# Transposing the recurrence's values step by step into a ring, and sharing slots between tiles

## The chip, the cores and the metric

The kernel runs on one core of one Trainium2 chip. The metric is the device time of one execution in microseconds. A core has five engines that each work through a queue of their own in order: TensorE (PE; its weight loads are shown as PEld), VectorE (DVE), ScalarE (ACT), GpSimd (POOL) and SyncE (SP), which here issues the weight transfers. Data lie in SBUF, in 128 partitions; matmuls write to PSUM, which has eight banks.

## What is computed

The reference runs four blocks over 256 latent tokens and 256 context tokens of width 1024, all in float32. The change touches the first one (layer 0): a modulated norm, an input projection, a mixer of differential attention and an RWKV recurrence, an output projection, and a squared-ReLU MLP, for latent and context tokens. The recurrence is run over the context first, forwards and backwards, and its two end states start that over the latent tokens:

```python
def step(S, inp):
    r_t, w_t, k_t, v_t, kk_t, a_t = inp
    sa = jnp.einsum('bhvk,bhk->bhv', S, kk_t)
    S = (S * w_t[:, :, None, :] - sa[..., None] * (kk_t * a_t)[:, :, None, :]
         + v_t[..., None] * k_t[:, :, None, :])
    return S, jnp.einsum('bhvk,bhk->bhv', S, r_t)
...
x = x + g1_l * (o_l.astype(x.dtype) @ w_out)
x = x + g2_l * _sq_relu_mlp(_ada(x, norm2, sh2_l, sc2_l), mlp_w1, mlp_w2)
if need_ctx:
    ctx = ctx + g1_c * (o_c.astype(ctx.dtype) @ w_out)
    ctx = ctx + g2_c * _sq_relu_mlp(_ada(ctx, norm2, sh2_c, sc2_c), mlp_w1, mlp_w2)
```

The context result goes on into layer 1; the following two blocks work on the latent tokens alone.

## The kernel before

Activations lie with their features on the partitions and 256 tokens along the row. A large product is three matmuls in a row for each 128x128 block of weights (`mm3`, lines 219 to 221): weights and activations are split into a high part in the format fp32r and a remainder, and high x high, high x low and low x high are added in PSUM. The weights come in pieces of 128x1024 (`w`, four buffers), which ScalarE rounds (`hi`, line 44) and VectorE subtracts (`lo`, line 45), 512 columns at a time.

The recurrence is computed in chunks of 64 tokens, two directions at once. `mixer(s)` in `layer0` is one call of it, for the context (s = 0) and for the latent tokens (s = 1). It has three parts. `rwkv_prep` makes decays and keys. `rwkv_inverse` builds a triangular 64x64 system for each chunk and head and solves it: a loop of 31 rounds of two dependent VectorE instructions (lines 456 and 458), with short matmuls before and after. Then come four steps: `rwkv_pre(j)` prepares step j without the state (exponentials, transposed keys `tok`, masked products `za` and `zr`), and `rwkv_step(j)` uses and updates the state `S`. `pre(j + 1)` is written ahead of `step(j)`. Last, `rwkv_out` and `rwkv_post` norm and gate the result for each of four feature tiles. `rwkv_values` transposes all values ahead of the first step: for each of four feature tiles and two directions it copies a tile into `vx` in chunk order, transposes it on TensorE, and copies the halves into `uv`, which holds all four chunks. A step writes its own results to the other half of `uv`.

In the order of the program layer 0 goes: context input projection, `mixer(0)`'s prep, latent norm, attention, `mixer(0)`'s rest, latent input projection with the token shift (`shifts`), context output projection (`w_out` on `xc`), `mixer(1)`, the context MLP, then the latent output projection (`w_out` on `xl`, with the operands of the latent MLP made in passing, `mlp_enter`), and, in layer 1, the latent MLP. Two MLPs (the latent ones of layers 0 and 1) run their first seven blocks on activations that are not yet normed; one block of the norm is made after each of these (`early` in `mlp`).

The instructions of each engine are put in order before the run, by a scheduler. It takes an instruction when its inputs, its engine and the memory of its output are free, and among several the one that stands first in the program; the first norm of an MLP has a raised priority. Memory is handed out in pools, from both ends of SBUF: in `mixer(1)` the pools `pl`, `q2` (keys, decays), `qx` (`X`, `vx`) and `up` (all of the steps) lie one above the other from below, `xc`, `xl` and then the MLP's pool from above. A pool is placed when it is opened, in the order of the program. Where it covers bytes of a pool that was closed, its tiles wait until the old tiles are done with. Within a pool, tiles with one tag share that tag's slots (`bufs`, one if not given) in turn, and a slot is as large as the largest of them. PSUM has three tags: `mm` (two banks), `sc` (two) and `po` (four).

Of the kernel before, what the change touches and what calls it, by code (L numbers as in the profile page):

```python
# [17 lines left out]
P = 128  # L18
# [57 lines left out]
class Kern:  # L76
# [114 lines left out]
        self.last = nc.scalar.activation(r, r, AF.Exp, scale=-0.5)  # L191
        return r

    def sumsq(self, pool, tiles, T, ones="ones", tag="sc"):

        nc = self.nc
        acc = None
        for t in tiles:
            sq = pool.tile([P, T], F32, tag="sq", name="sq", bufs=2)
            nc.scalar.activation(sq, t, AF.Square)  # L200
            if acc is not None:
                nc.vector.tensor_tensor(sq, sq, acc, op=ALU.add)
            acc = sq
        ps = self.psum(tag)
        nc.tensor.matmul(ps[:, :T], lhsT=self.C(ones), rhs=acc, start=True, stop=True)
        return ps[:, :T]
# [289 lines left out]

    HALF = [slice(0, 64), slice(64, 128)]

    def rwkv_values(self, vp, uv, v):

        nc = self.nc
        for p in range(4):
            for d in range(2):
                vx = vp.tile([P, 4, 64], F32, tag="vx", name="vx")
                lv = self.loc(v[p], d)
                x4 = vx.rearrange("p (a b) i -> p a b i", b=2)
                for b in range(2):
                    nc.vector.tensor_copy(x4[:, :, b, :], lv[:, :, 1 - b, :])
                pt = self.psum("sc")
                for a in range(2):  # L510
                    nc.tensor.transpose(pt[:, 128 * a : 128 * a + 128], vx[:, 2 * a : 2 * a + 2, :].rearrange("p c i -> p (c i)"), self.C("ident"))
                pv = pt[:, 0:256].rearrange("p (c x) -> p c x", x=128)
                for hf in range(2):
                    s = self.HALF[1 - hf]
                    nc.scalar.copy(uv[s, d, hf : 4 : 2, p, :], pv[s])

    def rwkv_pre(self, up, j, r, k, kk, ka, L):

        nc = self.nc
        g = lambda n, shape, bufs=2: up.tile([P] + shape, F32, tag=n, name=n, bufs=bufs)  # L520
        tok, zr, ar, za, el = g("tok", [2, 4, 128]), g("zr", [2, 4, 128]), g("ar", [2, 4, 128]), g("za", [4, 128]), g("el", [2, 4])
        for d, c in enumerate((j, 3 - j)):
            now, other = self.HALF[c & 1], self.HALF[1 - (c & 1)]
            loc = lambda t: t[:, :, 64 * c : 64 * c + 64][:, :, ::-1] if d else t[:, :, 64 * c : 64 * c + 64]
            lv = L[d][:, :, 64 * c : 64 * c + 64]
            ep, en = g("ep", [4, 65], 2), g("en", [4, 64], 1)
            nc.gpsimd.memset(ep[:, :, 0:1], 1.0)
            nc.scalar.activation(ep[:, :, 1:65], lv, AF.Exp)
            nc.scalar.activation(en, lv, AF.Exp, scale=-1.0)
            nc.gpsimd.tensor_copy(el[:, d, :], ep[:, :, 64])  # L530
            bk, A = g("bk", [4, 128], 1), ar[:, d]
            nc.vector.tensor_tensor(bk[:, :, now], loc(ka), en, op=ALU.mult)
            nc.gpsimd.tensor_tensor(A[:, :, other], loc(r), ep[:, :, 1:65], op=ALU.mult)
            nc.vector.tensor_tensor(bk[:, :, other], loc(k), en, op=ALU.mult)
            nc.vector.tensor_tensor(A[:, :, now], loc(kk), ep[:, :, 0:64], op=ALU.mult)
            pt = self.psum("sc")
            for p in range(4):
                nc.tensor.transpose(pt[:, 128 * p : 128 * p + 128], bk[:, p, :], self.C("ident"))
            nc.scalar.copy(tok[:, d], pt.rearrange("p (c x) -> p c x", c=4))
            pz = [self.psum("sc").rearrange("p (x c i) -> p x c i", x=2, c=4) for _ in range(2)]  # L540
            for p in range(4):
                for h, s in enumerate(self.HALF):
                    rhs = A[s, p, :].rearrange("p (a b) -> p a b", b=64)
                    nc.tensor.matmul(pz[h][:, :, p, :], lhsT=bk[s, p, :], rhs=rhs if c & 1 else rhs[:, ::-1, :], start=True, stop=True)  # L544
            for h, s in enumerate(self.HALF):
                mask = lambda n, rows: self.C(n)[rows].unsqueeze(1).broadcast_to([rows.stop - rows.start, 4, 64])
                nc.vector.tensor_tensor(za[other, :, s], pz[h][other, 1], mask("strict", other), op=ALU.mult)
                nc.vector.tensor_tensor(zr[:, d, :, s], pz[h][:, 0], mask("incl", slice(0, 128)), op=ALU.mult)
        return tok, zr, ar, za, el

    def rwkv_step(self, up, j, pre, uv, X, S, sy):


        nc = self.nc
        tok, zr, ar, za, el = pre
        ch = (j, 3 - j)

        ks, vs = [self.HALF[c & 1] for c in ch], [self.HALF[1 - (c & 1)] for c in ch]
# [11 lines left out]
        for q in range(2):  # L570
            for m, h, d in mhd:
                p, hs = 2 * q + m, self.HALF[h]
                nc.tensor.matmul(pp[q][ks[d], cols(d, m)][:, hs], lhsT=za[vs[d], p, hs], rhs=uv[vs[d], d, ch[d], p, hs],
                                 start=False, stop=True, skip_group_check=True)
            t = up.tile([P, 256], F32, tag="pn", name="pn", bufs=2)
            nc.scalar.mul(t[ks[0]], pp[q][ks[0], both(0)], -1.0)
            nc.vector.tensor_scalar(t[ks[1]], pp[q][ks[1], both(1)], -1.0, None, op0=ALU.mult)
            pn.append(t)
        for q in range(2):
            ps = self.psum("po")  # L580
            for m, h, d in mhd:
                i = (q * 2 + h) * 8 + (m * 2 + d) * 2 + ch[d] // 2
                o = slice(128 * m + 64 * h, 128 * m + 64 * h + 64)
                nc.tensor.matmul(ps[ks[d], o], lhsT=X[ks[d], i, :], rhs=pn[q][ks[d], o], start=True, stop=True, skip_group_check=True)
            for d in range(2):
                (nc.vector.tensor_copy if d else nc.scalar.copy)(uv[ks[d], d, ch[d], 2 * q : 2 * q + 2, :], ps[ks[d], 0:256].rearrange("p (m x) -> p m x", m=2))
        for q in range(2):
            ps = self.psum("po")
            pv = ps.rearrange("p (d m x) -> p d m x", m=2, d=2)
            for m, d in md:  # L590
                p = 2 * q + m
                nc.tensor.matmul(pv[:, d, m], lhsT=tok[:, d, p, :], rhs=uv[:, d, ch[d], p, :], start=True, stop=True, skip_group_check=True)
            for hs in self.HALF:
                s, e = S[hs, :, 2 * q : 2 * q + 2, hs], el[hs, :, 2 * q : 2 * q + 2]
                nc.vector.tensor_tensor(s, s, pv[hs, :, :, hs], op=ALU.add)
                nc.vector.tensor_tensor(s, s, e.unsqueeze(3).broadcast_to([64, 2, 2, 64]), op=ALU.mult)
        for q in range(2):
            for m, h, d in mhd:
                p, hs = 2 * q + m, self.HALF[h]
                nc.tensor.matmul(pp[q][vs[d], cols(d, m)][:, hs], lhsT=zr[:, d, p, hs], rhs=uv[:, d, ch[d], p, hs],  # L600
                                 start=False, stop=True, skip_group_check=True)
            for d in range(2):
                nc.scalar.copy(sy[vs[d], j, 256 * q : 256 * q + 256], pp[q][vs[d], both(d)])
# [16 lines left out]
    def rwkv_post(self, pool, y, r, k, v, gd, lora, p):  # L620
# [7 lines left out]
        d = pool.tile([P, 256], F32, tag="en", name="yd", bufs=1)  # L628
        nc.vector.scalar_tensor_tensor(d, ps[:, 0:256], -1.0 / 64, y, op0=ALU.mult, op1=ALU.add)
        nc.vector.tensor_tensor(t, ps[:, 256:512], v, op=ALU.mult)  # L630
        q = self.rstd(pool, self.sumsq(pool, [d], 256, "blk"), 64, 256, 2)
        nc.vector.tensor_tensor(d, d, q, op=ALU.mult)
        nc.vector.tensor_scalar(d, d, self.V("lnx_w")[:, p : p + 1], self.V("lnx_b")[:, p : p + 1], op0=ALU.mult, op1=ALU.add)
        nc.gpsimd.tensor_tensor(d, d, t, op=ALU.add)
# [4 lines left out]
    def layer0(self):  # L639
# [14 lines left out]
        mk = lambda n: [[g(pools[s], f"{n}{i}") for i in range(4)] for s in range(2)]  # L654
        v, oa = mk("v"), mk("oa")

        r4, k4 = [[g(pools[s], n, (P, 4, 256)) for s in range(2)] for n in ("r", "k")]
        r, k = [[[t[:, i, :] for i in range(4)] for t in x] for x in (r4, k4)]
# [18 lines left out]
        def mixer(s):  # L677
            with ExitStack() as D:
# [6 lines left out]
                    X = self.rwkv_inverse(pool("rp", E), qx, kk, ka, L)  # L685
                yield
                up = pool("up", D)
                uv, sy = g(up, "uv", (P, 2, 4, 4, 128)), g(up, "sy", (P, 4, 512))
                pre = lambda j: self.rwkv_pre(up, j, r4[s], k4[s], kk, ka, L)
                nxt = pre(0)  # L690
                self.rwkv_values(qx, uv, v[s])
                for j in range(4):
                    now, nxt = nxt, pre(j + 1) if j < 3 else None
                    self.rwkv_step(up, j, now, uv, X, S, sy)
# [105 lines left out]
    def mlp(self, l, mp, x, w, sm, h=None, done=None, side=(), tags=("mm", "mm")):  # L800
# [14 lines left out]
        for i in range(parts):  # L815
            u = []
            for n in range(m):
# [3 lines left out]
                b0 += 8  # L821
                if n % 4 == 2:
                    next(side, None)
                r = mp.tile([P, 256], F32, tag="relu", name="relu", bufs=2)
                if i == 0 and n < NF:
                    b = mp.tile([P, 1], F32, tag="bias", name="bias", bufs=2)
                    nc.vector.tensor_copy(b, ps[:, 256:257])
# [1002 lines left out]
```

## Time and profile before

| | us |
|---|---|
| median of 3 runs | 2097.12 (2091.21 to 2104.70) |
| the profiled execution | 2099.59 |
| its span, first to last instruction | 2097.8 |
| TensorE busy | 1928.2 |
| VectorE busy | 1425.8 |
| ScalarE busy | 1163.7 |
| GpSimd busy | 276.1 |

The profile is of one execution. A busy time is the time in which at least one instruction of that engine is on record as running; matmuls overlap, so their mean duration is longer than the distance at which they follow each other. Lines such as L45 are lines of the kernel before. A group of instructions is named by the tile written and the tiles read, `lo<-w,hi`. Each fp32 matmul shows as two records. The granted clock is TensorE's, as a share of 2.4 GHz; its other level is 1.2 GHz, shown as 0.50.

### The profile page before, as it was taken

To read this page: it belongs to the slowest core of one execution; us is meant where nothing else is said; L and a number is where in the kernel's file an instruction comes from. 1 tells how busy PE (TensorE), PEld (TensorE's weight loads), DVE (VectorE), ACT (ScalarE), POOL (GpSimd) and SP (SyncE) were. 2 spreads that over 40 slices of the span, in tenths; PEclk is the share of its full clock that TensorE was granted. 3 is DMA by queue.
4 is the path that set the end of the run, shared out by engine and by line. 5 is a ranking of instruction groups with operands and counts; after the bars stand their busy time and mean duration, and the time that the engine had idled before them with its cause. 6 is when DMAs were issued, how large, how long until landed. Compare 5 with 4: busy or idle time off the path is not lost.

```text
span 2097.8 us, 42380 instructions
## 1 busy us (share of the span) xinstructions
PE 1928.2 (92%) x16330; PEld 1739.4 (83%) x16330; DVE 1425.8 (68%) x2978; ACT 1163.7 (55%) x2543; POOL 276.1 (13%) x407
## 2 busy tenths in 40 slices
PE   5999999936989999999988989999999999999997
PEld 2986668715779999989855969999889999879997
DVE  3765866675666668557577988666777665677654
ACT  2554563533355568556463857666665555555553
POOL 1421120121010000000131030000003210103210
PEclk8999999965989999999998999999999999999999
DMA  8532541600025555676447515655424554224553
GB/s 280 169 120 72 180 138 35 205 28 1 1 93 182 184 184 193 223 241 206 150 146 236 175 67 167 193 188 183 161 92 140 182 185 167 81 101 141 182 187 114
DMA packets 91785, 313.26 MB, mean 149 GB/s; under 512 B 10304, under 2 KB 17728, under 8 KB 91584
## 3 DMA queue, kind: packets, MB, share of 16 engines
q1 hardware_dynamic: 83376, 299.94, 43.3%
q10 hardware_dynamic: 8208, 10.63, 1.6%
q8 instruction: 128, 2.10, 0.4%
q14 instruction: 73, 0.60, 0.1%
HBM read 309.48 MB, written 1.05 MB: 148 GB/s over the span
## 4 chain that ended last, share of the span: by engine, by line
PE 73%; DVE 11%; DMA 6%; ACT 5%; issue 2%; POOL 2%; ACTq 0%; POOLq 0%; SPq 0%; DVEq 0%
PE mm L219 15%; PE mm L220 15%; PE mm L221 15%; PE po L221 3%; PE po L220 3%; PE po L219 3%; DMA w<-in_mlp 2%; DMA w<-in_w_in 2%; DMA w<-in_mod 2%; PE sc L544 2%; PE mm L150 1%; DVE lo L45 1%; PE po L1391 1%; PE po L568 1%; ACT hi L44 1%
## 5 line engine op out<-in xcount | busy, mean ns | idle before, releaser
L45 DVE TENSOR_TENSOR lo<-w,hi 128x512 fp32r<-128x512 f32 x948 | 651.5, 693 | 294.6 <-ACT hi L44 272.4
L44 ACT CAST hi<-w 128x512 fp32r<-128x512 f32 x948 | 575.8, 618 | 425.0 <-PE mm L220 282.7
L219 PE MATMUL mm<-u_h,hi 128*128 128x256 f32 x1120 | 315.5, 282 | 4.0 <-ACT u_h L212 3.6
L220 PE MATMUL mm<-u_l,hi 128*128 128x256 f32 x1120 | 315.5, 282 | 0.2
L221 PE MATMUL mm<-u_h,lo 128*128 128x256 f32 x1120 | 315.2, 282 | 0.0
L219 PEld LDWEIGHTS mm<-u_h,hi 128*128 128x128 f32 x1120 | 212.6, 190 | 6.3 <-ACT u_h L212 4.0
L220 PEld LDWEIGHTS mm<-u_l,hi 128*128 128x128 f32 x1120 | 211.8, 189 | 0.5 <-DVE u_l L213 0.5
L221 PEld LDWEIGHTS mm<-u_h,lo 128*128 128x128 f32 x1120 | 211.9, 189 | 0.0
L150 PE MATMUL mm<-w,cs 128*32 128x256 f32 x640 | 70.6, 460 | 29.9 <-DMA w<-in_mod 29.6
L252 POOL TENSOR_SCALAR hf<-hf,g,mT 128x256 f32<-128x256 f32 x24 | 21.1, 879 | 473.8 <-ACT h1h L251 384.9
L1596 POOL TENSOR_TENSOR ut<-ut,gt 128x256 f32<-128x256 f32 x44 | 54.0, 1226 | 197.8 <-ACT hi L44 173.6
L150 PEld LDWEIGHTS mm<-w,cs 128*32 128x32 f32 x640 | 18.5, 118 | 60.1 <-DMA w<-in_mod 39.3
L213 DVE TENSOR_TENSOR u_l<-relu,u_h 128x256 fp32r<-128x256 f32 x96 | 40.7, 425 | 34.4 <-ACT u_h L212 34.4
L343 POOL TENSOR_SCALAR sht<-shf,mu 128x256 f32<-128x256 f32 x28 | 37.8, 1348 | 112.5 <-ACT shf L341 112.4
L219 PE MATMUL mm<-h0h,hi 128*128 128x256 f32 x130 | 40.2, 312 | 12.2 <-ACT h0h L251 6.1
L212 ACT CAST u_h<-ut 128x256 fp32r<-128x256 f32 x44 | 17.9, 406 | 58.2 <-POOL ut L1596 58.2
L213 DVE TENSOR_TENSOR u_l<-ut,u_h 128x256 fp32r<-128x256 f32 x44 | 18.7, 425 | 43.8 <-ACT u_h L212 43.8
L1548 POOL TENSOR_TENSOR xl<-xl,yy 128x256 f32<-128x256 f32 x16 | 14.2, 890 | 228.9 <-DVE yy L1547 228.9
L219 PEld LDWEIGHTS mm<-h0h,hi 128*128 128x128 f32 x130 | 25.0, 194 | 20.9 <-ACT h0h L251 7.4
L832 ACT ACTIVATE relu<-relu 128x256 f32<-128x256 f32 x96 | 39.9, 417 | 4.0 <-DVE h7l L253 1.5
L221 PE MATMUL mm<-h0h,lo 128*128 128x256 f32 x130 | 38.7, 298 | 3.5 <-DVE lo L45 3.5
L68 POOL TENSOR_TENSOR sq<-sq 128x256 f32<-128x256 f32 x24 | 20.9, 870 | 158.9 <-ACT sq L60 156.5
(1125 smaller groups left out, 6177.1 us busy)
## 6 DMA issues: line engine op xcount, KB each, us to landing
w<-in_mlp SPq DMA_DIRECT2D x192, 512.0 KB, 4.5
w<-in_w_in SPq DMA_DIRECT2D x102, 512.0 KB, 4.1
w<-in_mod SPq DMA_DIRECT2D x96, 512.0 KB, 5.7
w<-in_ffn_in SPq DMA_DIRECT2D x88, 512.0 KB, 3.7
w<-in_ffn_out SPq DMA_DIRECT2D x44, 512.0 KB, 4.5
w<-in_w_out SPq DMA_DIRECT2D x40, 512.0 KB, 4.3
w<-in_memkv SPq DMA_DIRECT2D x8, 512.0 KB, 3.8
xc<-in_ctxT ACTq DMA_DIRECT2D x16, 128.0 KB, 5.9
```

What stands on the lines that cost most here:

```text
L44: nc.scalar.copy(self.hi, w)
L45: nc.vector.tensor_tensor(self.lo, w, self.hi, op=ALU.subtract)
L150: nc.tensor.matmul(ps[32 * j : 32 * j + 32, o : o + 256], lhsT=self.cs[:, k, :], rhs=w[:, 256 * j : 256 * j + 256], start=(k == 0), stop=( ...
L213: nc.vector.tensor_tensor(lo, src, hi, op=ALU.subtract)
L219: nc.tensor.matmul(out, lhsT=wh, rhs=xh, start=start, stop=False)
L220: nc.tensor.matmul(out, lhsT=wh, rhs=xl, start=False, stop=False)
L221: nc.tensor.matmul(out, lhsT=wl, rhs=xh, start=False, stop=stop)
L252: (nc.gpsimd if k % 2 else nc.vector).tensor_scalar(t, t, scale, bias, op0=ALU.mult, op1=ALU.add)
L343: nc.gpsimd.tensor_scalar(t, f[:, 1:257], self.mu1[:, i : i + 1], None, op0=ALU.mult)
L544: nc.tensor.matmul(pz[h][:, :, p, :], lhsT=bk[s, p, :], rhs=rhs if c & 1 else rhs[:, ::-1, :], start=True, stop=True)
L832: nc.scalar.activation(r, r, AF.Square)
L1596: nc.gpsimd.tensor_tensor(w, w, t, op=ALU.mult)
```

## The change

The values are no longer transposed ahead of the steps. `rwkv_values` is gone. `rwkv_pre(j)` copies the values of its own two chunks to `vx`, transposes them in four matmuls into one bank of `sc`, and copies each direction's half to `uv`. `uv` now holds one step's chunks and has two slots in turn. Besides, slots are shared: in the post-work `sq` goes into the slots of `za` and `rstd` into that of `vx`, both in `up`, and the MLP's `relu` goes into the two slots of `hf`. `vx` moves from the pool `qx` to `up`, where it is twice as large. `v` becomes one tile of 128x4x256 for each `s`, of the same size as the four before. Indexing of `uv` by chunk falls away.

```diff
-    def sumsq(self, pool, tiles, T, ones="ones", tag="sc"):
+    def sumsq(self, pool, tiles, T, ones="ones", tag="sc", sq="sq"):
...
-            sq = pool.tile([P, T], F32, tag="sq", name="sq", bufs=2)
-            nc.scalar.activation(sq, t, AF.Square)
+            x = pool.tile([P, T], F32, tag=sq, name="sq", bufs=2)
+            nc.scalar.activation(x, t, AF.Square)
...
-    def rwkv_values(self, vp, uv, v):
-
-        nc = self.nc
-        for p in range(4):
-            for d in range(2):
-                vx = vp.tile([P, 4, 64], F32, tag="vx", name="vx")
-                lv = self.loc(v[p], d)
-                x4 = vx.rearrange("p (a b) i -> p a b i", b=2)
-                for b in range(2):
-                    nc.vector.tensor_copy(x4[:, :, b, :], lv[:, :, 1 - b, :])
-                pt = self.psum("sc")
-                for a in range(2):
-                    nc.tensor.transpose(pt[:, 128 * a : 128 * a + 128], vx[:, 2 * a : 2 * a + 2, :].rearrange("p c i -> p (c i)"), self.C("ident"))
-                pv = pt[:, 0:256].rearrange("p (c x) -> p c x", x=128)
-                for hf in range(2):
-                    s = self.HALF[1 - hf]
-                    nc.scalar.copy(uv[s, d, hf : 4 : 2, p, :], pv[s])
-
-    def rwkv_pre(self, up, j, r, k, kk, ka, L):
+    def rwkv_pre(self, up, j, r, k, v, kk, ka, L):
...
+        uv, vx = g("uv", [2, 4, 128]), g("vx", [4, 128], 1)
         for d, c in enumerate((j, 3 - j)):
...
+            nc.vector.tensor_copy(vx[:, :, other], loc(v))
...
+        pt = self.psum("sc")
+        for p in range(4):
+            nc.tensor.transpose(pt[:, 128 * p : 128 * p + 128], vx[:, p, :], self.C("ident"))
+        for d, c in enumerate((j, 3 - j)):
+            s = self.HALF[1 - (c & 1)]
+            nc.scalar.copy(uv[s, d], pt[s].rearrange("p (c x) -> p c x", c=4))
+        return tok, zr, ar, za, el, uv
...
-        q = self.rstd(pool, self.sumsq(pool, [d], 256, "blk"), 64, 256, 2)
+        q = self.rstd(None, self.sumsq(pool, [d], 256, "blk", sq="za"), 64, 256, 2, pool.tile([P, 256], F32, tag="vx", name="rstd"))
...
-                uv, sy = g(up, "uv", (P, 2, 4, 4, 128)), g(up, "sy", (P, 4, 512))
-                pre = lambda j: self.rwkv_pre(up, j, r4[s], k4[s], kk, ka, L)
+                sy = g(up, "sy", (P, 4, 512))
+                pre = lambda j: self.rwkv_pre(up, j, r4[s], k4[s], v4[s], kk, ka, L)
                 nxt = pre(0)
-                self.rwkv_values(qx, uv, v[s])
                 for j in range(4):
...
-                r = mp.tile([P, 256], F32, tag="relu", name="relu", bufs=2)
+                r = mp.tile([P, 256], F32, tag="hf", name="relu", bufs=2)
```

## Rows read from the trace of the kernel before

**Rows 1.** The page's part 1: busy time, share of the span, instructions.

```profile
PE 1928.2 (92%) x16330; PEld 1739.4 (83%) x16330; DVE 1425.8 (68%) x2978; ACT 1163.7 (55%) x2543; POOL 276.1 (13%) x407
```

**Rows 2.** The page's part 4: shares of the chain that ended last.

```profile
PE 73%; DVE 11%; DMA 6%; ACT 5%; issue 2%; POOL 2%; ACTq 0%; POOLq 0%; SPq 0%; DVEq 0%
```

**Rows 3.** Busy time by stretch: length, PE, PEld, DVE, ACT, POOL (instructions), clock, DMA share, GB/s.

```profile
209.00:260.00 51.00, 47.60 (x322) 33.13 (x320) 45.18 (x138) 28.90 (x76) 7.65 (x10) 1.00 0.55 184
...
294.00:383.00 89.00, 88.10 (x882) 74.71 (x880) 58.19 (x149) 37.37 (x93) 12.32 (x28) 0.96 0.19 62
...
430.00:490.00 60.00, 13.63 (x480) 10.68 (x482) 42.76 (x99) 14.69 (x28) 9.41 (x20) 0.52 0.01 1
455.00:479.00 24.00, 0.00 (x0) 0.00 (x0) 21.84 (x64) 0.00 (x0) 0.00 (x0) 0.50 0.00 0
490.00:590.00 100.00, 85.83 (x797) 70.71 (x792) 58.04 (x151) 38.36 (x97) 11.46 (x28) 0.77 0.01 1
...
590.00:604.00 14.00, 9.93 (x48) 8.02 (x48) 11.72 (x35) 6.36 (x13) 3.40 (x4) 0.77 0.15 44
...
650.00:750.00 100.00, 100.00 (x836) 100.00 (x835) 63.80 (x105) 61.84 (x127) 0.00 (x0) 1.00 0.58 184
```

**Rows 4.** Timeline of ScalarE, 426 to 432 us: start, length, instruction.

```profile
430.65 0.40 ACT L191 ACTIVATE rs<-rs 128x256 f32<-128x256 f32 x1
```

**Rows 5.** Timeline around the end of `mixer(1)`, and at the end of the context MLP.

```profile
589.57 0.42 DVE L637 TENSOR_TENSOR r<-sc,yd 128x256 f32<-128x256 f32 x1 [0.90 <-POOL yd L634]
...
590.03 0.76 DVE L249 TENSOR_TENSOR hf<-xc,rs 128x256 f32<-128x256 f32 x2
...
786.11 0.48 DVE L776 SCALAR_TENSOR_TENSOR xl<-mm,mT,xl 128x256 f32<-128x256 f32 x1 [0.15 <-PE mm L221]
```

**Rows 6.** Busy time of one line, 294 to 383 us: line 219 (220, 221 alike), line 150.

```profile
294.00:383.00 89.00, 10.28 (x32) 6.31 (x32) 0.96 0.19 62
...
294.00:383.00 89.00, 3.59 (x38) 1.00 (x38) 0.96 0.19 62
```

**Rows 7.** Timeline of VectorE in `mixer(1)`'s solve, two of its 62 instructions.

```profile
465.85 0.42 DVE L456 TENSOR_TENSOR tm<-ai,T 128x255 f32<-128x255 f32 x1
466.31 0.42 DVE L458 TENSOR_TENSOR T<-T,tm 128x255 f32<-128x255 f32 x1
```

**Rows 8.** Timeline of VectorE in `mixer(0)`'s solve: first, three between, last.

```profile
209.61 0.19 DVE L456 TENSOR_TENSOR tm<-ai,T 128x31 f32<-128x31 f32 x1
...
244.50 0.38 DVE L456 TENSOR_TENSOR tm<-ai,T 128x231 f32<-128x231 f32 x1
...
244.87 0.68 DVE L45 TENSOR_TENSOR lo<-w,hi 128x512 fp32r<-128x512 f32 x1
245.47 0.39 DVE L458 TENSOR_TENSOR T<-T,tm 128x231 f32<-128x231 f32 x1
...
259.66 0.19 DVE L458 TENSOR_TENSOR T<-T,tm 128x31 f32<-128x31 f32 x1
```

**Rows 9.** Timeline of TensorE: first and last of the eight transpose groups, `mixer(1)`.

```profile
503.30 0.41 PE L511 MATMUL sc<-c_cst,vx 128*128 128x128 f32 x2 [0.19 <-DVE zr L548]
...
511.67 0.69 PE L511 MATMUL sc<-c_cst,vx 128*128 128x128 f32 x2
```

**Rows 10.** Groups, 432 to 590 us: busy us, mean ns of one, idle time before.

```profile
L515 ACT COPY uv<-sc 64x256 f32<-64x256 f32 x16 | 5.9, 366 | 4.8 <-PE sc L511 4.6
...
L539 ACT COPY tok<-sc 128x512 f32<-128x512 f32 x8 | 4.7, 585 | 2.9 <-PE sc L538 2.7
...
L508 DVE COPY vx<-v 128x128 f32<-128x128 f32 x16 | 4.2, 306 | 3.0 <-PE sc L511 3.0
```

**Rows 11.** Instructions on the tile `relu`: least, median, largest ns; first, last start us.

```profile
L213 DVE TENSOR_TENSOR u_l<-relu,u_h x96: 414/425/524, 605.8 to 1424.9; 128x256 fp32r<-128x256 f32 x96
...
L829 ACT ACTIVATE relu<-relu,bias x14: 493/508/513, 813.0 to 1308.1; 128x256 f32<-128x256 f32 x14
```

**Rows 12.** Groups on GpSimd: 294 to 383 us, then 490 to 590 us.

```profile
L533 POOL TENSOR_TENSOR ar<-r,ep 128x256 f32<-128x256 f32 x7 | 5.3, 770 | 10.4 <-PE sc L544 8.0 <-PE po L568 2.4
...
L533 POOL TENSOR_TENSOR ar<-r,ep 128x256 f32<-128x256 f32 x8 | 6.1, 769 | 10.2 <-PE sc L544 6.8 <-PE po L568 3.4
```

More of the change, by code (lines that the diff above doesn't have):

```diff
@@ L198, in sumsq @@
         for t in tiles:
-            sq = pool.tile([P, T], F32, tag="sq", name="sq", bufs=2)
-            nc.scalar.activation(sq, t, AF.Square)
+            x = pool.tile([P, T], F32, tag=sq, name="sq", bufs=2)
+            nc.scalar.activation(x, t, AF.Square)
             if acc is not None:
-                nc.vector.tensor_tensor(sq, sq, acc, op=ALU.add)
-            acc = sq
+                nc.vector.tensor_tensor(x, x, acc, op=ALU.add)
+            acc = x
         ps = self.psum(tag)
@@ L548, in rwkv_pre, with rwkv_step @@
                 nc.vector.tensor_tensor(zr[:, d, :, s], pz[h][:, 0], mask("incl", slice(0, 128)), op=ALU.mult)
-        return tok, zr, ar, za, el
-    def rwkv_step(self, up, j, pre, uv, X, S, sy):
+        pt = self.psum("sc")
[5 more added lines that the diff above has]
+        return tok, zr, ar, za, el, uv
+    def rwkv_step(self, up, j, pre, X, S, sy):
         nc = self.nc
-        tok, zr, ar, za, el = pre
+        tok, zr, ar, za, el, uv = pre
         ch = (j, 3 - j)
@@ L572, in rwkv_step @@
                 p, hs = 2 * q + m, self.HALF[h]
-                nc.tensor.matmul(pp[q][ks[d], cols(d, m)][:, hs], lhsT=za[vs[d], p, hs], rhs=uv[vs[d], d, ch[d], p, hs],
+                nc.tensor.matmul(pp[q][ks[d], cols(d, m)][:, hs], lhsT=za[vs[d], p, hs], rhs=uv[vs[d], d, p, hs],
                                  start=False, stop=True, skip_group_check=True)
@@ L585, in rwkv_step @@
             for d in range(2):
-                (nc.vector.tensor_copy if d else nc.scalar.copy)(uv[ks[d], d, ch[d], 2 * q : 2 * q + 2, :], ps[ks[d], 0:256].rearrange("p (m x) -> p m x", m=2))
+                (nc.vector.tensor_copy if d else nc.scalar.copy)(uv[ks[d], d, 2 * q : 2 * q + 2, :], ps[ks[d], 0:256].rearrange("p (m x) -> p m x", m=2))
         for q in range(2):
@@ L591, in rwkv_step @@
                 p = 2 * q + m
-                nc.tensor.matmul(pv[:, d, m], lhsT=tok[:, d, p, :], rhs=uv[:, d, ch[d], p, :], start=True, stop=True, skip_group_check=True)
+                nc.tensor.matmul(pv[:, d, m], lhsT=tok[:, d, p, :], rhs=uv[:, d, p, :], start=True, stop=True, skip_group_check=True)
             for hs in self.HALF:
@@ L599, in rwkv_step @@
                 p, hs = 2 * q + m, self.HALF[h]
-                nc.tensor.matmul(pp[q][vs[d], cols(d, m)][:, hs], lhsT=zr[:, d, p, hs], rhs=uv[:, d, ch[d], p, hs],
+                nc.tensor.matmul(pp[q][vs[d], cols(d, m)][:, hs], lhsT=zr[:, d, p, hs], rhs=uv[:, d, p, hs],
                                  start=False, stop=True, skip_group_check=True)
@@ L653, in layer0 @@
         pools = [pool("pc", LC, "right"), pool("pl", LL)]
[L654 to L658, printed above, removed]
+        oa = [[g(pools[s], f"oa{i}") for i in range(4)] for s in range(2)]
+        r4, k4, v4 = [[g(pools[s], n, (P, 4, 256)) for s in range(2)] for n in ("r", "k", "v")]
+        r, k, v = [[[t[:, i, :] for i in range(4)] for t in x] for x in (r4, k4, v4)]
         wa, gd = [g(pools[s], "wa") for s in range(2)], [g(pools[s], "gd") for s in range(2)]
@@ L687, in mixer @@
                 up = pool("up", D)
-                uv, sy = g(up, "uv", (P, 2, 4, 4, 128)), g(up, "sy", (P, 4, 512))
-                pre = lambda j: self.rwkv_pre(up, j, r4[s], k4[s], kk, ka, L)
+                sy = g(up, "sy", (P, 4, 512))
+                pre = lambda j: self.rwkv_pre(up, j, r4[s], k4[s], v4[s], kk, ka, L)
                 nxt = pre(0)
-                self.rwkv_values(qx, uv, v[s])
                 for j in range(4):
                     now, nxt = nxt, pre(j + 1) if j < 3 else None
-                    self.rwkv_step(up, j, now, uv, X, S, sy)
+                    self.rwkv_step(up, j, now, X, S, sy)
                 for p in range(4):
```

## The prediction

> **What bounds the kernel now.** I read the page first, for the shares of the span: TensorE has work on record for 92% of it [rows 1], and the chain of work that ended last lies on TensorE for 73% [rows 2]. So time is won where TensorE waits. Next I read the table of stretches [rows 3] for where that is. In the middle of the context MLP (650 to 750 us) TensorE is busy all the time, at the full clock of 1.00, with 836 matmuls in 100 us, 0.1196 us each. From 430 to 490 us it has 13.6 of 60 us, and from 455 to 479 nothing at all, at a granted clock of 0.50, which is the lower of its two levels; from 490 to 590 it shows 85.8 us, but at a mean clock of 0.77. The transfers stand still there too (share 0.01). This is the second call of the recurrence, `mixer(1)`: its inverse (to 490) and its four steps with their post-work (to 590). VectorE is the busy one in the inverse, with 42.8 us.
>
> Then I looked for work that could have filled this hole. The context MLP needs only `xc` and the factor `rs`, and `rs` is finished at 431 us [rows 4]. Yet its first instruction, `hf<-xc,rs`, runs at 590.03, right behind the last instruction of `mixer(1)` at 589.57 [rows 5]. No data ties it to `mixer(1)`; memory does. In the compiled program of before, `up` ends at byte 179,424 of a partition and the MLP's pool begins at byte 176,032, so 3,392 bytes are shared: the MLP's `g2`, `h0h`, `h0l` and both `hf` lie on `pn`, `sq` and `rstd`, which the post-work uses to the end.
>
> **What the change moves in memory.** By the tile shapes (four bytes a value): `uv` goes from one 16,384-byte tile to two of 4,096, which saves 8,192; `vx` moves from `qx` (1,024) into `up` as 2,048; `sq` (2 x 1,024) and `rstd` (1,024) go into the slots of `za` and `vx`. `up` shrinks by 9,216 and starts 1,024 lower, so it ends at 169,184. The MLP loses `relu` (2 x 1,024) and begins at 178,080. That leaves 8,896 bytes free, and nothing of the MLP waits for `mixer(1)` any more. Its PSUM tag (`mm`) is not one of the recurrence's (`sc`, `po`), and its weights need a DMA share of 0.58 where 0.01 is used [rows 3]. So I expect the MLP to start at about 432.
>
> **What that is worth.** Before, from 430 to 604 (when the MLP runs without gaps) 174 us pass, and 48 MLP matmuls are done in them [rows 3], 5.7 us worth. So 168.3 us are not MLP time. After, these become the part of the inverse and of the steps in which TensorE does no MLP matmul.
>
> *Steps and post-work.* `mixer(0)` ran them beside fillers: 294 to 383, 89 us [rows 3], in which TensorE also did 32 matmuls each of lines 219, 220 and 221 and 38 of line 150 [rows 6]. That is 96 x 0.1196 = 11.5 us plus 3.6 us, so the steps took 89 - 15 = 74 us net, at a mean clock of 0.96. Alone, in `mixer(1)`, they took 100 us at 0.77. I take 74; the far bound is 100 (nothing fits in).
>
> *Inverse.* Here VectorE decides. The inverse's 62 solve instructions follow each other alone (0.46 us from start to start [rows 7]), some 24 us from 455 to 479. In `mixer(0)`, where the attention and the shifts ran beside it, the same 62 ran from 209.6 to 259.9, 50 us, with single foreign instructions between them, among them the split of weights `lo` of the shifts, which stand later in the program [rows 8]. So an MLP instruction can get in between two solve instructions. I take the same stretch: 60 + 26 = 86 us, and 8 more for the MLP's own norm, 20 VectorE instructions of about 0.4 us, which are given a high priority: 94 us. VectorE was 45.18/51 = 0.886 busy in that part of `mixer(0)` [rows 3]; at that share 83.3 us, less the mixer's 42.8 and the norm's 8, leave 32.5. An MLP microsecond on TensorE needs 0.638 us of VectorE (63.8 in 100 us [rows 3]), so 51 us of MLP run within the inverse, and 94 - 51 = 43 us do not. Bounds: if the solve is not stretched, 68 us at 0.886 leave 9.4, 15 us of MLP, 53 not; if it is stretched and VectorE is never idle, 43 leave 68 us of MLP, 26 not.
>
> Sum: 168.3 - 74 - 43 = 51 us won, with 41 and 68 by the two inverse bounds, and 51 - 26 = 25 if the steps gain nothing. Scarcely any of it can be lost later: the MLP's successor, the output projection of the latent tokens (first `xl` at 786.1 [rows 5]), follows the MLP and would start that much sooner; TensorE is full on both sides of the border.
>
> **The other edits.** The values: before, 16 rounds of transposes in eight groups run at the head of the steps (503.30 to 511.67 [rows 9]). 16 transposes stay 16. ScalarE's 16 copies of 64x256 at 0.366 us (5.9 us) become 8 of 64x512, for which the nearest row is a copy of 128x512 at 0.585 (4.7); VectorE's 16 copies of 128x128 at 0.306 become 8 of 128x256, between that and twice that [rows 10]. Per `mixer` -1 us of ScalarE and -2.4 to 0 of VectorE, both beside a full TensorE: nothing. The serial head of 8.4 us shrinks to one group per step; once TensorE is filled by the MLP this is hidden, so I take 0, and keep 8 us of gain for the range. Against it, `sc` serves 28 tiles a call in place of 32, but seven in each `rwkv_pre` where it was six, between two buffers; what waits there is hidden under the same filler and is part of the 25 to 100 us above.
>
> The shared `hf`/`relu` ring touches the two MLPs with early blocks, seven blocks each. A `relu` goes through five instructions of at most 0.524 us [rows 11], 2.6 us, while the next block's 24 matmuls take 2.87. So with one slot instead of two it still fits: 0. If `relu` and `hf` had to alternate strictly, 2 x 2.6 - 2.87 = 2.3 us for each of 14 blocks, 33 us: a bound for the range, and not likely, as each keeps its own of the two slots. `sq` and `rstd` in foreign slots: `za` and `vx` are idle in the post-work; 0.
>
> A row bears on VectorE and GpSimd working at once: `ar<-r,ep` on GpSimd took 770 ns beside the shifts' weight splits in `mixer(0)` and 769 in `mixer(1)` [rows 12]. The Trainium skill ("SBUF — State Buffer", "Summary: rules for kernel authors") says that a VectorE instruction with two SBUF inputs and a reading GpSimd instruction block each other fully. By that rule each of the eight `ar` and eight `be` could wait for one 0.69 us split, 11 us, and 2058 would come out; the trace shows no such lengthening, and the sum leaves it out.
>
> **Rivals.**
> 1. *Starved filler* (gain under 23 us). The solve keeps VectorE and the steps stay as slow as alone: 168.3 - 100 - 53 = 15 us, 2082. For it: VectorE 21.8 of 24 us in the solve [rows 3]. Against it: the `lo` between solve instructions in `mixer(0)` [rows 8].
> 2. *The order does not change*: the queues are fixed before the run, and if the MLP is put behind `mixer(1)` anyway, only the values' head can be won: 2089 to 2097. Against it: in `mixer(0)` later work was drawn forward wherever its memory allowed [rows 6, 8].
> 3. *Slower: `mixer(1)` becomes the last to end.* Each engine works its queue in order; MLP instructions ahead of the recurrence's delay its chain, and the projection of `xl` needs its result. It decides when `mixer(1)` ends after the MLP, and makes the kernel slower by over 1% from an end at 786 + 21 = 807 on, 376 us after 431 where it now takes 159. In `mixer(0)` solve to end took 383 - 209.6 = 173 us, against 590 - 455.5 = 134.5: a factor of 1.29, an end at 635. At a factor of 2.5 it would end at 431 + 398 = 829, 43 us later than the projection starts now, and the time would be 2140.
>
> **How the numbers follow.** The profiled execution spans 2097.8 us and took 2099.6; the median of the runs is 2097.1. I set the gain of 51, less 1 for small losses, against the median: 2047. Likeliest case, the MLP beside `mixer(1)` with a gain of 23 to 73 us: 0.80. More than 73 us (as the values' head adds to the upper bound): 0.03. Rival 1: 0.07, nearly all of it within 1%. Rival 2: 0.06. Rival 3: 0.04. The range runs from 2024 (68 and part of the head) to 2073 (steps gain nothing). About 1% (21 us) is what a measurement of this kernel can tell from no change: faster 0.84, same 0.12, slower 0.04.
>
> **What would show it.** Right: `h0h` and MLP matmuls begin at 431 to 440 and run through the solve; the granted clock between 455 and 530 is 1.00 where it was 0.50; the solve takes 40 to 60 us; `mixer(1)` ends between 600 and 640; the first `xl` of the projection comes at about 735. Wrong: no MLP matmul before `mixer(1)` ends (rival 2, the memory account fails); TensorE still empty through the solve (rival 1, inverse term); idle TensorE after the last MLP matmul with `mixer(1)` still running (rival 3); TensorE waiting for `relu` in the early blocks of the latent MLPs (ring term).

## The result and the profile after

| | us | ratio to before, 95% interval |
|---|---|---|
| before, median of 4 runs | 2100.1 (2091.21 to 2104.70) | |
| after, median of 4 runs | 2038.9 (2036.7 to 2044.0) | 0.9717 [0.9678, 0.9756] |
| predicted | 2047 (2024 to 2073) | |

The profiled execution of after took 2037.99 us and spans 2036.2. The kernel became 61 us faster where 50 were forecast. The mechanism is the forecast one, but three terms of the sum were off and partly cancelled: the overlap with the inverse gave 15 us more, that with the steps 3 us less, and the slots that `relu` now shares with `hf`, which I had costed at nothing, cost 5 us.

The context MLP now begins as soon as its norm is known, inside `mixer(1)`. The first fence is the timeline of all engines (start, length, instruction), to be read beside [rows 4] and [rows 5].

```profile
428.47 0.40 ACT L191 ACTIVATE rs<-rs 128x256 f32<-128x256 f32 x1
...
428.90 0.76 DVE L249 TENSOR_TENSOR hf<-xc,rs 128x256 f32<-128x256 f32 x2
...
430.06 0.47 PE L219 MATMUL mm<-h0h,hi 128*128 128x256 f32 x2
...
611.63 0.42 DVE L628 TENSOR_TENSOR r<-sc,yd 128x256 f32<-128x256 f32 x1 [0.52 <-POOL yd L625]
...
719.79 0.48 DVE L765 SCALAR_TENSOR_TENSOR xl<-mm,mT,xl 128x256 f32<-128x256 f32 x1 [0.15 <-PE mm L221]
```

`hf<-xc,rs` follows `rs` by 0.4 us where it stood 159 us behind it. `mixer(1)` ends at 612.05, 22 us later than before, and nobody waits for it: the latent output projection delivers its first `xl` only at 719.79, 66 us sooner than at 786.11.

The second fence has busy time by stretch (length, PE, PEld, DVE, ACT, POOL, granted clock, DMA share, GB/s); it answers to [rows 3]. The first line is the start of the inverse with the MLP's norm, the second holds the solve, the third is the whole inverse, the fourth the steps and the post-work, the last the MLP alone.

```profile
428.00:453.00 25.00, 19.46 (x217) 15.55 (x218) 21.80 (x51) 17.61 (x41) 10.76 (x20) 0.82 0.14 44
453.00:505.00 52.00, 51.71 (x511) 49.89 (x511) 48.54 (x118) 28.94 (x59) 2.75 (x4) 0.92 0.50 159
428.00:516.00 88.00, 80.87 (x960) 74.76 (x961) 77.14 (x174) 54.38 (x112) 13.52 (x24) 0.88 0.36 115
516.00:612.00 96.00, 92.48 (x984) 80.98 (x979) 68.92 (x168) 48.87 (x116) 12.64 (x28) 1.00 0.13 40
612.00:700.00 88.00, 88.00 (x736) 88.00 (x735) 60.33 (x112) 55.17 (x112) 0.00 (x0) 1.00 0.57 184
```

TensorE, which stood still in the solve at a clock of 0.50, is busy for 51.7 of 52 us there, at 0.92; in the steps the clock is 1.00 where it was 0.77. How much MLP that is, the matmuls of line 219 tell (220 and 221 have as many, give or take a few); the lines are 428 to 453, 453 to 505, 505 to 516, the whole inverse, and the steps.

```profile
428.00:453.00 25.00, 8.92 (x29) 6.32 (x29) 0.82 0.14 44
453.00:505.00 52.00, 36.68 (x128) 24.82 (x128) 0.92 0.50 159
505.00:516.00 11.00, 4.46 (x13) 2.99 (x13) 0.84 0.22 71
428.00:516.00 88.00, 50.06 (x168) 34.13 (x168) 0.88 0.36 115
516.00:612.00 96.00, 16.11 (x54) 10.14 (x54) 1.00 0.13 40
```

At 0.1196 us a matmul the inverse holds 3 x 168 = 504 of them, 60.3 us of MLP, so 88 - 60.3 = 27.7 us of it are not MLP. The steps hold about 160, 19.1 us, and 96 - 19.1 = 76.9 are not MLP. With the 168.3 us of before that makes 168.3 - 27.7 - 76.9 = 63.7 us. The distance from the norm's `rs` to the first `xl` shrank by 64.2.

### The profile page after: what moved, and what is told of

Its sections match the earlier page's. It is cut to its first block, busy times and chain, and to the rows that moved or that the text cites. A ratio compares the mean times of both kernels' runs of the same rounds, so it can differ in the third digit from the quotient of the medians.

```text
span 2036.2 us, 42319 instructions
## 1 busy us (share of the span) xinstructions
PE 1914.3 (94%) x16330; PEld 1727.5 (85%) x16330; DVE 1417.9 (70%) x2962; ACT 1160.3 (57%) x2527; POOL 276.1 (14%) x407
## 4 chain that ended last, share of the span: by engine, by line
PE 74%; DVE 11%; DMA 5%; ACT 5%; issue 3%; POOL 2%; ACTq 0%; POOLq 0%; DVEq 0%; SPq 0%
PE mm L220 16%; PE mm L219 16%; PE mm L221 16%; PE po L220 3%; PE po L221 3%; PE po L219 3%; DMA w<-in_mlp 2%; DVE lo L45 2%; DMA w<-in_mod 2%; PE sc L528 1%; DMA w<-in_w_in 1%; PE po L1380 1%; PE mm L150 1%; ACT hi L44 1%; PE po L1443 1%
```

## How the kernels are compared

Single runs of one kernel lie up to 25 us apart, and part of that comes before the change can act: the start of `rs` lies between 420 and 435 us in the profiles. With relu slots of its own (a run below) each engine has the same order of instructions up to the latent MLP as in the changed kernel, and yet `rs` starts at 435.19 against 428.47. So beside the times I compare distances within the profiles: R is the start of `rs` after the context projection, U the first `xl` of the latent output projection, V the first sum of the latent MLP of layer 0 into `xl`, E the span. Each ratio is to runs of the kernel before on the same chip; their median lay between 2091.7 and 2100.1 us, so medians of different kernels are compared only where the text says that they ran side by side.

| kernel | MLP starts, after R | last of `mixer(1)` starts, after R | U - R | V - U | E - V | ratio to before | median |
|---|---|---|---|---|---|---|---|
| before | 159.4 | 159 | 355.5 | 49.9 | 1261.8 | | |
| after | 0.4 | 183 | 291.3 | 54.7 | 1261.7 | 0.9717 | 2038.9 |
| e2_slots_only | 0.4 | 185 | 290.6 | 55.0 | 1260.0 | 0.9724 | 2032.2 |
| e3_no_fit | 152.2 | 152 | 348.4 | 54.9 | 1261.9 | 1.0052 | 2101.9 |
| e4_after_inverse | 60.7 | 164 | 332.7 | 54.7 | 1263.0 | 0.9956 | 2082.7 |
| e6_more_vector | 0.4 | 204 | 292.3 | 55.1 | 1258.5 | 0.9739 | 2041.2 |
| e7_before_more_vector | 172.3 | 172 | 368.4 | 49.9 | 1255.8 | 1.0055 | 2105.5 |
| e1_relu_own | 0.4 | 184 | 292.3 | 49.9 | 1257.3 | 0.9742 | 2038.3 |
| e1b_relu_own | 0.4 | 185 | 293.0 | 49.9 | 1263.6 | 0.9701 | 2030.9 |
| a1_after | 0.4 | 185 | 292.9 | 55.0 | 1260.8 | 0.9725 | 2038.9 |
| e5_hf4 | 0.4 | 180 | 288.4 | 48.8 | 1263.0 | 0.971 | 2032.9 |
| a2_after | 0.4 | 182 | 290.4 | 54.7 | 1263.0 | 0.9751 | 2043.2 |
| e8_best | 0.4 | 184 | 290.7 | 50.0 | 1258.2 | 0.9686 | 2030.0 |

U - R of kernels that do the same there agrees within 3 us and V - U within 0.4; E - V scatters over 8 us without a pattern.

## Experiments

### Is it the fit, and the fit alone?

Theory: the gain comes because the steps' pool and the MLP's no longer share bytes. The ring is one way to get there; the shared slots alone free 5,120 bytes, more than the 3,392 of the overlap. So `e2_slots_only` is the kernel before with its values still transposed ahead of the loop, and only these edits (with the argument `sq` of `sumsq`, as in the change):

```diff
...
-        q = self.rstd(pool, self.sumsq(pool, [d], 256, "blk"), 64, 256, 2)
+        q = self.rstd(None, self.sumsq(pool, [d], 256, "blk", sq="za"), 64, 256, 2, pool.tile([P, 256], F32, tag="bk", name="rstd"))
...
-                r = mp.tile([P, 256], F32, tag="relu", name="relu", bufs=2)
+                r = mp.tile([P, 256], F32, tag="hf", name="relu", bufs=2)
```

> The kernel before with nothing but slots shared: sq in the slots of za, rstd in that of bk, relu in those of hf. The values are transposed ahead of the steps as before. That frees 5,120 bytes where 3,392 overlapped, so the context MLP's pool lies clear of up by 1,728. Theory (the fit is what brings the time): MLP matmuls begin at some 430 us and the whole takes 2035 to 2050, ratio 0.970 to 0.977. Rival (the values' ring brings a good part, its serial head was 8.4 us in each call): 2050 to 2060 if it counts for one call, and about 2100 if the fit alone does nothing.

`e3_no_fit` is the opposite: the changed kernel with a block of 12,288 bytes in `up` that nothing uses, so that the overlap is 3,392 bytes again.

```diff
+                if s:
+                    nc.gpsimd.memset(g(up, "pad", (P, 3072))[:, 0:1], 0.0)
                 sy = g(up, "sy", (P, 4, 512))
```

> The changed kernel with an unused block of 12,288 bytes per partition in up for the latent call, so that up and the MLP's pool overlap over 3,392 bytes again, by the same tile pn among others; all other edits stay. Theory (the fit is what brings the time): the MLP starts behind the latent call, 2090 to 2105, ratio 0.995 to 1.003 (the values' head gives back up to 8 us, the shared hf and relu cost 4.7). Rival (the ring of values or the slots bring it): 2040 to 2070.

Measured: e2 0.9724 [0.9685, 0.9764] with U - R = 290.6, the whole gain without the ring; e3 1.0052 [1.0029, 1.0076] with U - R = 348.4, a ratio a little above the 0.995 to 1.003 that I expected. Below is e3's timeline at the end of `mixer(1)`, then its table of stretches for the inverse and for the steps.

```profile
586.14 0.42 DVE L628 TENSOR_TENSOR r<-sc,yd 128x256 f32<-128x256 f32 x1 [0.90 <-POOL yd L625]
...
586.60 0.76 DVE L249 TENSOR_TENSOR hf<-xc,rs 128x256 f32<-128x256 f32 x2
```

```profile
434.00:494.00 60.00, 13.81 (x487) 10.80 (x488) 41.97 (x96) 14.45 (x28) 9.40 (x20) 0.52 0.01 1
494.00:586.00 92.00, 76.90 (x790) 64.25 (x784) 56.78 (x144) 37.16 (x89) 10.99 (x29) 0.89 0.01 1
```

The MLP again starts right behind the last instruction of `mixer(1)`, and the inverse is as empty as in [rows 3]. So the fit is the cause. What the ring itself is worth shows only here: without the fit, the steps take 92 us instead of 100, because the serial head of the values is gone, and U - R is 355.5 - 348.4 = 7.1 us shorter. The place fits: counted from the end of the solve, the last `pn` of the first step starts at 31.5 us in e3 and at 39.1 in before, and the later steps keep 7 us of that. I had put that at up to 8, and as hidden once the MLP runs; e2, which still has the head, agrees (290.6 against 291.3).

### Which part of the gain lies where

`e4_after_inverse` is the changed kernel with an unused block in the inverse's pool, so that the MLP's memory is taken until the inverse is done.

```diff
-                    X = self.rwkv_inverse(pool("rp", E), qx, kk, ka, L)
+                    rp = pool("rp", E)
+                    if s:
+                        nc.gpsimd.memset(g(rp, "pad", (P, 8896))[:, 0:1], 0.0)
+                    X = self.rwkv_inverse(rp, qx, kk, ka, L)
```

> The changed kernel with an unused block of 35,584 bytes in the pool of the latent call's inverse, so that the MLP's first tiles lie on the inverse's last tile xd and the MLP can start only when the inverse is done, at some 490 us; steps and post-work stay free of it. This splits the gain. Theory by the rows of after (steps and post-work 77 us net of MLP where they took 100 alone; the rest of the 64 us falls to the inverse): about 23 us, plus some for the MLP's own start, of which 8 us of waiting are then hidden by the first step: 2070 to 2080, ratio 0.985 to 0.991. Rival (the steps were full before and give nothing, all lies in the inverse): 2095 and more.

The MLP starts 60.7 us behind R, and U - R is 332.7. So, from before to after: 7.1 us for the head (355.5 to 348.4), 15.7 for overlap with the steps (348.4 to 332.7), and 41.4 for overlap with the inverse (332.7 to 291.3). The fence has two stretches of e4. The first holds the end of its solve (to 474.4), in which TensorE does nothing, and the short matmuls behind it, which begin at 476.6; the second is the middle of the steps.

```profile
455.00:482.00 27.00, 3.85 (x128) 3.60 (x128) 22.88 (x53) 3.74 (x4) 0.00 (x0) 0.50 0.00 1
...
560.00:600.00 40.00, 37.74 (x313) 34.80 (x313) 28.93 (x72) 24.50 (x59) 3.25 (x4) 1.00 0.27 84
```

The timed gain of e4, 0.9956 [0.9932, 0.998] or 9 us, is smaller than I expected (0.985 to 0.991) and than its distances say: 22.8 us won up to U less 4.8 up to V are 18.0. What the other 9 us are is not settled; the scatter before R and behind V is of that size.

### Is VectorE what limits the MLP in the inverse?

My sum rested on that. If it holds, more VectorE work in the solve must cost MLP time. `e6_more_vector` is the changed kernel with the first instruction of each solve round issued twice in `mixer(1)` (its result stays the same); `e7_before_more_vector` has the same edit in the kernel before.

```diff
-            nc.vector.tensor_tensor(m, ai[:, s + 1 :, s : s + 1].broadcast_to([P, n, s + 1]),
-                                    T[:, s : s + 1, : s + 1].broadcast_to([P, n, s + 1]), op=ALU.mult)
+            for _ in range(1 + self.twice):
+                nc.vector.tensor_tensor(m, ai[:, s + 1 :, s : s + 1].broadcast_to([P, n, s + 1]),
+                                        T[:, s : s + 1, : s + 1].broadcast_to([P, n, s + 1]), op=ALU.mult)
...
+                self.twice = s
```

> The changed kernel with the first of the two instructions of each solve round issued twice in the latent call, 31 more VectorE instructions that compute the same values again, 10.5 us of VectorE by the rows of before. Theory (in the changed kernel TensorE is the one that is full in the inverse, and the MLP takes up what the solve is stretched by): rs to projection grows by 0 to 4 us. Rival (VectorE sets the pace of the inverse there, as the prediction's sum had it: each of its microseconds is one of MLP work lost): it grows by 10 us or more.

> The kernel before with the same 31 extra VectorE instructions in the latent call's solve. Control for the run on the changed kernel, where 21 us more of solve left rs to projection at 292.3 us. Theory (in the kernel before nothing runs beside the solve, so each of its microseconds is one of the whole): rs to projection grows by 10 to 13 us, from 355.5 to 366 to 368, the time by as much, ratio some 1.005. Rival (the extra instructions are absorbed there too, so the run on the changed kernel shows nothing): 355 to 358.

In e7 the 31 instructions cost what they take: U - R grows by 12.9 us. In e6 the solve ends 97.5 us behind R where it ended at 76.4, and `mixer(1)` ends 21 us later, yet U - R is 292.3 against 290.4 to 292.9 in the changed kernel. e6's stretch of the solve, and then the matmuls of line 219 over its whole inverse:

```profile
456.00:529.00 73.00, 72.58 (x672) 70.53 (x672) 68.15 (x169) 43.09 (x89) 2.76 (x4) 0.92 0.53 161
```

```profile
431.50:540.00 108.50, 65.43 (x224) 44.06 (x224) 0.92 0.42 128
```

TensorE stays full. The longer inverse simply holds more MLP: 3 x 224 x 0.1196 = 80.4 of 108.5 us, which leaves 28.1 that are not MLP, against 27.7 in after. So VectorE, busy for 68.15 of 73 us, does not limit the MLP in the solve; TensorE, with 72.58, is the full engine. This step of my prediction falls.

### What does the shared ring of `hf` and `relu` cost?

V - U had grown from 49.9 to 54.7 us, in the latent MLP of layer 0, where I had seen no cost. `e1_relu_own` and `e1b_relu_own` (the same kernel timed twice, the second time beside `a1_after`, the unaltered changed kernel) give `relu` its own two slots back; the pools still fit.

```diff
-                r = mp.tile([P, 256], F32, tag="hf", name="relu", bufs=2)
+                r = mp.tile([P, 256], F32, tag="relu", name="relu", bufs=2)
```

> The changed kernel with one edit undone: the MLP's relu has two slots of its own again, so hf and relu no longer take turns. The pool still lies clear of up. Theory (the shared slots hold the norm of the latent MLP of layer 0 back): before, 23.7 us pass from the first relu at 812.3 to the first sum into xl at 836.0; after the change 28.5, from 746.0 to 774.5. So this stretch goes back to 24 us, the whole to some 2034, 0.9775 times the changed kernel's lead kept plus 4.7 us, that is a ratio to before of 0.968 to 0.970. Rival (the 4.7 us come from elsewhere, the order of weight loads for one): the stretch stays at 28 us and the time at 2039, ratio 0.972.

> The changed kernel with two slots of its own for relu, once more, now beside the changed kernel. Theory (the shared slots cost 4.9 us in the latent MLP of layer 0, and the rest of the kernel does not give them back): 4 to 8 us under the changed kernel of this call, projection to latent MLP 49 to 51 us. Rival (what is won there is waited for later): no difference of the times beyond 2 us.

> The changed kernel once more, unaltered, beside the next three on one chip. Two profiles of kernels with the same queues up to the latent MLP had the factor rs 6.7 us apart, so single spans differ by that much without any edit; stretches are therefore measured from rs on. Every theory: rs to the first sum of the projection 290 to 293 us, from there to the first sum of the latent MLP 54 to 56 us; the time 2036 to 2044.

V - U is 49.9 us in both, and 55.0 in a1. It is 48.8 to 50.0 in all six kernels with own slots and 54.7 to 55.1 in all seven with shared ones. The timeline of VectorE shows how: first the start of this MLP in after, then in before.

```profile
745.99 0.42 DVE L817 TENSOR_TENSOR relu<-mm,rs 128x256 f32<-128x256 f32 x1
746.32 0.42 DVE L249 TENSOR_TENSOR hf<-xl,rs 128x256 f32<-128x256 f32 x1
...
749.31 0.42 DVE L213 TENSOR_TENSOR u_l<-relu,u_h 128x256 fp32r<-128x256 f32 x1
749.65 0.42 DVE L817 TENSOR_TENSOR relu<-po,rs 128x256 f32<-128x256 f32 x1
749.98 0.42 DVE L249 TENSOR_TENSOR hf<-xl,rs 128x256 f32<-128x256 f32 x1
...
751.86 0.42 DVE L253 TENSOR_TENSOR h1l<-hf,h1h 128x256 fp32r<-128x256 f32 x1 [0.80 <-POOL hf L252]
752.32 0.42 DVE L817 TENSOR_TENSOR relu<-mm,rs 128x256 f32<-128x256 f32 x1
```

```profile
812.31 0.42 DVE L828 TENSOR_TENSOR relu<-mm,rs 128x256 f32<-128x256 f32 x1
812.64 0.42 DVE L249 TENSOR_TENSOR hf<-xl,rs 128x256 f32<-128x256 f32 x1
...
813.04 0.41 DVE L828 TENSOR_TENSOR relu<-po,rs 128x256 f32<-128x256 f32 x1
813.37 0.41 DVE L249 TENSOR_TENSOR hf<-xl,rs 128x256 f32<-128x256 f32 x1
```

With shared slots the second `relu` comes 3.7 us behind the first, after the first one's last reader `u_l`; with its own it comes 0.7 us behind. The third stands right behind `h1l`, the last reader of the `hf` before it. A `relu` and the `hf` that follows it fill the two slots, and the next `relu` comes only when one of them has had its last reader. So each of the seven early blocks waits for the one before, and the seven `relu` take 19.9 us from first to last (745.99 to 765.85) where they took 16.3 (812.31 to 828.65). The operands that `hf` becomes are late in turn, and TensorE waits for both. The fence is TensorE's waits in after, 745 to 780 us (who waits for whom, us in total, times, longest).

```profile
PE mm L219 <- ACT u_h L212: 1.9, 1, 1.9
PE po L219 <- ACT h5h L251: 0.4, 1, 0.4
```

In times, e1 gives 0.9742 [0.9707, 0.9778], no better than after and not the 0.968 to 0.970 that I expected, and e1b 2030.9 against a1's 2038.9, with intervals that overlap. 5 us is at the edge of what the times tell apart; the distance shows it in every profile.

`e5_hf4` is e1b with four slots for `hf` in the norms of these MLPs; the free 8,896 bytes have room for them.

```diff
-                t = pool.tile([P, 256], F32, tag="hf", name="hf", bufs=2)
+                t = pool.tile([P, 256], F32, tag="hf", name="hf", bufs=4 if pool.name == "mlp" else 2)
```

> relu with two slots of its own and hf with four in the MLPs of layer 0, which together take 4,096 of the 8,896 free bytes. Theory (the start of the context MLP waits in a chain over the two hf slots: from rs on its norm takes 13 us, in which TensorE stands still some 6): with four slots the norm runs ahead and rs to projection shrinks by 2 to 5 us, the time by as much against the kernel with its own relu. Rival (VectorE's work, not the slots, spaces the norm): rs to projection stays at 291 to 293.

U - R is 288.4, some 2 to 5 us under the others, and V - U 48.8; the time, 2032.9, is not told apart from e1b's 2030.9. That the norm's start is a little tight is suggested, not shown.

### A version without the costs

`e8_best` starts from e2 (values ahead of the loop), gives `relu` its own slots, and finds the missing bytes by putting the staging tile `vx` into the slots of the steps' `pn`, of which there are two. 704 bytes are left between the pools.

```diff
-                vx = vp.tile([P, 4, 64], F32, tag="vx", name="vx")
+                vx = vp.tile([P, 4, 64], F32, tag="pn", name="vx", bufs=2)
...
-                self.rwkv_values(qx, uv, v[s])
+                self.rwkv_values(up, uv, v[s])
```

> The kernel before with its values still transposed ahead of the loop, the three shared slots of the changed kernel except the one of relu, which keeps slots of its own, and the staging tile of the values in the slots of the step's pn. That leaves 704 bytes between the steps' pool and the latent MLP's. Theory (the fit alone brings the gain; the ring costs some 5 us in the first call before the context projection's norm; the shared slots of relu cost some 5 us in the latent MLP of layer 0): first latent projection 291 us after the norm's rs, V minus U 49.9 us, the norm's rs some 305 us after kss, time some 2029 us and some 10 us under the changed kernel in the same call. Rival (ring and shared slots cost nothing, the differences seen were of the profiles alone): the time of the changed kernel, 2037 to 2041 us.

> The changed kernel as it is, for a comparison with the version that beats it, if the theory holds: 2038 us, first latent projection 291 to 293 us after rs, V minus U 55 us, rs 309 us after kss.

e8 takes 2030.0 us, 0.9686 [0.9648, 0.9723], beside a2 with 2043.2, 0.9751 [0.9721, 0.9782]: 13 us faster than the changed kernel by the medians, with intervals that just overlap. About 5 of these are V - U, 50.0 against 54.7. Busy time by stretch around the seven early blocks, e8 first, then after:

```profile
744.00:776.00 32.00, 31.96 (x262) 31.23 (x261) 29.16 (x72) 29.03 (x62) 2.98 (x8) 1.00 0.57 187
```

```profile
745.00:777.00 32.00, 28.63 (x215) 26.65 (x214) 26.31 (x65) 27.66 (x58) 2.68 (x8) 0.97 0.47 154
```

TensorE is full in e8 and misses 3.4 us in after. The rest of the 13 us is not placed. I had expected it in the first call: from the logarithm on `kss` in `mixer(0)` to R, three profiles with the values ahead have 302.6, 305.4 and 305.7 us, and nine with the ring 308.6 to 312.6, as if the ring cost `mixer(0)` and the context projection some 5 us. But e8 has 308.6, beside a2's 308.9. A cost of the ring there is not confirmed, and that part of the expectation missed. It is not excluded either. Set the change of the medians against the change of the distances up to V: for the kernels without the ring (e2, e7, e8) the two agree within 2 us. Of those with it, after, a1 and e1b agree as well, but e6 and e5 come out 4 and 6 us slower than their distances say, and e1, e3, e4 and a2 8 to 12. If that is a price of the ring, it lies outside these stretches, and no run here shows where.

## Why the prediction was right, and where its steps were not

- **The empty place and its reason** (nothing but 3,392 shared bytes holds the MLP back): right. e3 puts them back and loses the gain, e2 wins it without the ring.
- **Steps, 74 us not MLP**, from `mixer(0)` beside fillers: 76.9. A stretch where the same code already runs beside other work was a good measure. The far bound of 100 was too far, as it held the head of the values: e3 has 92.
- **Inverse, 43 us not MLP**: 27.7. This is the mis-sized term, and the step that failed is "Here VectorE decides". I took VectorE's 0.886 in `mixer(0)` [rows 3] for a ceiling, but there TensorE was the fuller engine (47.6 of 51 us). In the solve of after VectorE reaches 48.54 of 52 us. I also set durations of single instructions against a union of times. In after, VectorE's 174 instructions from 428 to 516 last 87.8 us by their sum and 77.14 by the clock, because records that stand back to back overlap. The value fell near my other bound, 26 (VectorE never idle). That the solve lengthens was right (463.85 to 504.8, 41 us; I said 50), but the length did not matter, as e6 shows: TensorE was full all along. About half of what is lost lies at the start, where 25 us hold 85 MLP matmuls (10.2 us) at a clock of 0.82, so 14.8 of the 27.7 us.
- **The ring of `hf` and `relu`, 0**: wrong, 5 us. What failed is the 2.6 us for the five instructions of a `relu`. I added up their durations; but other work stands between them on VectorE and ScalarE, and from the start of a `relu` to the end of its `u_l` the first takes 3.74 us (745.99 to 749.73) and the seven 2.4 to 4.1. Six of the seven are longer than the 2.87 us of the next block's matmuls, so one slot is not enough. Strict alternation of the two tiles, my bound of 2.3 us for each of 14 blocks, did not come either: the next `relu` takes whichever slot is done with. In the second MLP with early blocks the seven `relu` take 19.3 us with own slots and 19.4 with shared ones, so little could be lost there; what spaces them was not tested.
- **Values, 0, and up to 8 us for the head**: the head is 7.1 us without the fit and hidden with it, as said. e3's 1.0052 shows that the ring without the fit gains nothing in time; of its price only the shared slots' 5 us are placed.
- **VectorE and GpSimd at once**: the eight `ar` on GpSimd take 891 ns on the mean in the steps of after against 769 [rows 12], the eight `be` 820 against 764. That is 8 x 0.122 + 8 x 0.056 = 1.4 us in a call, so leaving it out of the sum was right by its size. "No such lengthening" was wrong: behind the two equal means of [rows 12] stand single `ar` of 0.67 to 0.95 us. Where two such instructions meet in after, one lasts until the other is done:

```profile
456.53 0.97 POOL L431 TENSOR_TENSOR be<-ka,en 128x256 f32<-128x256 f32 x1 [1.84 <-PE sc L440]
456.83 1.22 DVE L45 TENSOR_TENSOR lo<-w,hi 128x512 fp32r<-128x512 f32 x1
...
520.40 1.66 POOL L517 TENSOR_TENSOR ar<-r,ep 128x256 f32<-128x256 f32 x1
...
520.85 0.67 DVE L45 TENSOR_TENSOR lo<-w,hi 128x512 fp32r<-128x512 f32 x1
```

  That `lo` lasts 1.22 us instead of 0.68 and ends 0.55 behind the `be`; that `ar` lasts 1.66 instead of 0.68 and ends 0.54 behind the `lo`. The rule of the Trainium skill ("SBUF — State Buffer", "Summary: rules for kernel authors") is that the second of two such instructions to issue blocks until the first has finished. The trace agrees with it for the `lo`; the `ar`, by its record, started ahead of its `lo` and yet ended behind it. My 11 us were too high because I let each of the sixteen meet a `lo`, where four do for more than 0.1 us.
- **Rivals**: neither the starved filler nor the unchanged order came. `mixer(1)` ends at 612 where I had worked out some 635 and where 807 would have decided. The mark for the clock (1.00 from 455 to 530) was set too high: 453 to 505 has 0.92.

The sum as measured: 63.7 us in the place of 51, less 4.8 for the ring of `hf` and `relu`, makes 59 between R and E, where the profiles differ by 59.5. That the forecast came so near is in part luck: the 15 us too few for the inverse were half made up by the 3 too many for the steps and the 5 of the ring.

## What to carry to other kernels

Where an engine stands idle beside work that needs none of the current results, look at the addresses: a few thousand shared bytes can hold back a whole stage, and an unused block that restores the overlap tests it. Free the bytes from tiles whose slots lie idle, and not from two tiles of a running loop that would then share their slots. Whether one slot is enough is told by the time from a tile's first writer to the end of its last reader as a trace has it, not by a sum of durations. To size an overlap, ask which engine is full in the stretch that serves as the model; a busy share of another engine there is no ceiling, and a doubled instruction tests it.

## What the runs showed of the hardware

Records of back-to-back VectorE instructions overlap. In after two `lo`, each of which lasts 0.68 us alone (as in [rows 8]), take 1.28 us together:

```profile
746.72 1.28 DVE L45 TENSOR_TENSOR lo<-w,hi 128x512 fp32r<-128x512 f32 x2
```

TensorE's granted clock differs with what fills the solve. In e4, from 455 to 482, where TensorE does nothing until 476.6 and then has the inverse's short matmuls, it is 0.50, the lower level; in after, with the MLP's matmuls all through, it is 0.92 over the solve and 1.00 in the steps behind it.
